# The diagonal of a recurrence's score matrix: from GpSimd products and two-column sums instead of full products

## The chip, the cores and the metric

The kernel runs on one core of a Trainium2 chip. The metric is the device time of one execution in microseconds (us). Engines are named as in the profile: PE is TensorE (matmuls; PEld its weight loads), DVE is VectorE, ACT is ScalarE, POOL is GpSimd, and SP is SyncE, whose queue issues most of the transfers. A tile of 128x512 has 128 partitions and 512 elements in each. PSUM is the memory that PE writes, SBUF the one that holds the operands.

## The reference

The program is two transformer blocks in a row on 512 tokens of width 1024, in float32. The first block mixes tokens by a stick-breaking attention and by a gated linear recurrence (HGRN2), then goes through a two-level mixture of 16 experts; the second has retention, a differential attention, a cross-attention and a dense feed-forward layer. The change concerns the recurrence alone. With eight heads of 64 key and 64 value elements, it is

```
cum = jnp.cumsum(gc, axis=2)                       # gc: log of the forget gate, in a chunk
diff = cum[:, :, :, None, :] - cum[:, :, None, :, :]
decay = jnp.exp(jnp.where(causal[:, :, None], diff, -jnp.inf))
scores = jnp.einsum('bhtk,bhsk,bhtsk->bhts', qc, kc, decay)
o = (jnp.einsum('bhts,bhsv->bhtv', scores, vc)
     + jnp.einsum('bhtk,bhkv->bhtv', qc * jnp.exp(cum), state))
```

The score of a query at t and a key at s is a sum over the key elements of q times k times a decay that differs for each element. On the diagonal, s = t, the decay is 1, and the score is the plain inner product of q and k at that token.

## The kernel before, in words

The program is written as one function, `body`; a scheduler then puts the instructions of each engine in a fixed order, and each engine works its own list from the front. An instruction that waits holds everything behind it on that engine. So a change of one operation can move others in the lists, and the order below is what the scheduler made of both programs.

The recurrence works on blocks of 128 tokens, four of them, and on pairs of heads, four pairs (`hgrn_pair(t)`, called for t = 0 to 3). A pair of heads fills the 128 partitions: head h holds partitions 64h to 64h + 63. For a pair, `hk[t]` holds the keys and `hc[t]` the running sums of the log gates, both 128x512; `hq[2t]` and `hq[2t + 1]` hold the queries of the two heads, each 128x512 with the other head's partitions filled with zeros, so that a product over 128 partitions gives one head alone.

The score matrix of a pair, transposed, is the tile `std`: 128 key positions, then 2 heads, 4 blocks and 128 query positions. It is built in two steps. First the diagonal: the lines 490 to 496 do, for each head, four full 128x128 products of keys and queries on PE into one PSUM bank, and VectorE multiplies the bank by the identity matrix `ident`, so that only the diagonal stays and the rest of `std` is zero. This product also gives the tile its zeros. Second, seven levels (m = 1, 2, 4, ..., 64) fill what lies under the diagonal. A level takes the decay against a reference position: VectorE makes the differences `e` (L506, L508), ACT their exponentials (L509, L512), VectorE the scaled keys `KT` (L510, L513) and the scaled queries `QT` (L516), PE multiplies them (L520), and the parts that belong to this level are put into `std`: by VectorE with a predicated copy (L523) for the first five levels, by ACT (L530) for the last two. After the levels come the state (L538 to L562), the output (L568, L570), and a norm over each head (L573 to L577, with the helper lines 311, 312, 319, 266 and 267).

The weights of all projections come through `split` (L180 to L183): a transfer on SP's queue into a buffer, then ACT rounds it (L182) and VectorE makes the rest (L183); three products of such parts (L200 to L202) stand for one exact product. While the recurrence runs, the scheduler puts pieces of the next projections (v, q and k of the stick-breaking attention) between its products on PE.

In this stretch GpSimd has eight fills with zeros (L591) and nothing else. PSUM tiles with the tag "at" share four banks here; `std` has two buffers.

Of the kernel before, what the change touches and what calls it, by code (L numbers as in the profile page):

```python
# [8 lines left out]
F32 = mybir.dt.float32  # L9
# [11 lines left out]
S = 512  # L21
# [62 lines left out]
def body(tc, a, out):  # L84
    nc = tc.nc
    V, A, T, G = nc.vector, nc.scalar, nc.tensor, nc.gpsimd
    es = ExitStack()

    def pool(name, bufs, side=None, space=None, stack=None):
        kw = {}  # L90
        if side:
            kw["side"] = side
        if space is not None:
            kw["space"] = space
        return (stack or es).enter_context(tc.tile_pool(name=name, bufs=bufs, **kw))
# [21 lines left out]
    def psum(tag, name="ps"):  # L117
        if tag == "at":
            return banks[1][0].tile([128, 512], F32, name=name, tag="at", bufs=banks[1][1])
        return ps.tile([128, 512], F32, name=name, tag=tag, bufs=2)  # L120
# [48 lines left out]
    ident = cp.tile([128, 128], F32, name="ident")  # L169
# [161 lines left out]
    ones64 = ones64r.bitcast(F32)  # L331
# [80 lines left out]
    at = ExitStack()  # L412
# [10 lines left out]
    hg = pool("hg", 1, side="right", stack=hgst)  # L423
# [9 lines left out]
    hq, hk, hc, hv = {}, {}, {}, {}  # L433
# [48 lines left out]
    def blocks(ap):  # L482
        return ap.rearrange("p (b t) -> p b t", b=4)
# [3 lines left out]
    def hgrn_pair(t):  # L487
        std = hg.tile([128, 2, 4, 128], F32, name="std", bufs=2)
        cum, k = hc[t], hk[t]
        tot = [cum[:, b * 128 + 127:b * 128 + 128] for b in range(4)]  # L490
        for h in range(2):
            o = blocks(psum("at"))
            for b in range(4):
                T.matmul(o[:, b, :], k[:, b * 128:(b + 1) * 128], hq[2 * t + h][:, b * 128:(b + 1) * 128],
                         start=True, stop=True)
            V.tensor_mul(std[:, h], o, ident[:, None, :].to_broadcast([128, 4, 128]))
        for lev, m in enumerate((1, 2, 4, 8, 16, 32, 64)):
            i = turn[0] % 2
            turn[0] += 1
# [14 lines left out]
            for h in range(2):  # L514
                p_ = slice(64 * h, 64 * h + 64)
                V.tensor_mul(Q_[p_, h, :].rearrange("p (g i) -> p g i", i=m),  # L516
                             halves(hq[2 * t + h], m)[p_, :, 1, :], ev[p_, :, 1, :])
            o = psum("at").rearrange("p (h t) -> p h t", h=2)
            for b in range(4):
                T.matmul(o[:, :, b * 64:(b + 1) * 64], K_[:, b * 128:(b + 1) * 128], Q_[:, :, b * 64:(b + 1) * 64],  # L520
                         start=True, stop=True)
# [23 lines left out]
        for h in range(2):  # L545
            p_ = slice(64 * h, 64 * h + 64)
# [9 lines left out]
        for b in range(3):  # L556
            for h in range(2):
                p_ = slice(64 * h, 64 * h + 64)
# [5 lines left out]
        o = psum("tp")  # L564
        for b in range(4):
# [3 lines left out]
            for h in range(2):  # L569
                T.matmul(o[64 * h:64 * h + 64, cc], hv[b][:, (2 * t + h) * 64:(2 * t + h + 1) * 64], std[:, h, b, :],  # L570
                         start=(b == 0), stop=(b == 3))
# [8 lines left out]
    for t in range(4):  # L580
        hgrn_pair(t)
# [880 lines left out]
```

## Time and profile before

| | us |
|---|---|
| median of 3 runs (1622.94 to 1624.32) | 1623.21 |
| the profiled execution | 1623.13 |
| its span, first to last instruction | 1621.3 |
| PE busy in the span | 1579.7 |
| DVE busy in the span | 955.9 |
| ACT busy in the span | 831.6 |
| POOL busy in the span | 75.2 |

The profiled execution's time is 1.8 us more than its span. The granted clock of PE was 0.998 of full speed over the run. A matmul is modelled as lasting longer than the time to the next one, since they are pipelined; that is why busy shares of PE near 100% do not say by themselves that PE is the bound, and why this document goes by what waits for what.

### The profile page before, as it was taken

The numbers are of one execution on the slowest core, as the hardware profiler recorded it, in microseconds if no ns is written. First come the engines' busy times: TensorE is split into PE (matmuls) and PEld (weight loads), VectorE is DVE, ScalarE is ACT, GpSimd is POOL, SyncE is SP. The second block draws the span as 40 slices with busy tenths as digits, with TensorE's granted clock in tenths as the row PEclk, the third lists the DMA queues.
The fourth block names the chain that finished last, engine by engine and source line by source line (L and its number), as shares of the span: only waits on it lengthen the run. The fifth ranks groups of instructions, "written<-read, shape, count | busy, mean of one in ns | idle before, by whom it ended". The sixth has DMA issues, their size and how long they took to land. (4 is left out here: it accounts for less than half of the span.)

```text
span 1621.3 us, 20374 instructions
## 1 busy us (share of the span) xinstructions
PE 1579.7 (97%) x7631; PEld 1223.8 (75%) x7631; DVE 955.9 (59%) x1485; ACT 831.6 (51%) x1331; POOL 75.2 (5%) x92
## 2 busy tenths in 40 slices
PE   7999999999999999999989999999999999999999
PEld 6887776668878777776667667657878888888887
DVE  6459945643647899998855766456555433333221
ACT  5445556665335888888865664434444322323120
POOL 3000000000001211111110000000000000000000
PEclk9999999999999999999999999999999999999999
DMA  7230121123469999999974204224211333332331
GB/s 227 72 104 27 53 79 39 48 67 119 143 231 317 310 369 368 357 365 368 380 263 135 75 15 130 75 58 142 90 53 54 115 91 105 91 103 92 97 124 39
DMA packets 203070, 242.88 MB, mean 150 GB/s; under 512 B 10400, under 2 KB 133560, under 8 KB 202968
## 3 DMA queue, kind: packets, MB, share of 16 engines
q1 hardware_dynamic: 188800, 205.43, 38.1%
q0 software_dynamic: 7056, 24.27, 5.3%
q10 hardware_dynamic: 7112, 11.85, 2.5%
q8 instruction: 61, 1.00, 0.2%
q14 instruction: 41, 0.34, 0.1%
HBM read 223.69 MB, written 15.73 MB: 148 GB/s over the span
## 5 line engine op out<-in xcount | busy, mean ns | idle before, releaser
L183 DVE TENSOR_TENSOR wlo<-wraw,whi 128x1024 fp32r<-128x1024 f32 x210 | 256.0, 1223 | 284.9 <-ACT whi L182 275.5
L182 ACT CAST whi<-wraw 128x1024 fp32r<-128x1024 f32 x210 | 220.5, 1051 | 392.9 <-PE ps L201 276.2
L200 PE MATMUL ps<-hTh,whi 128*128 128x512 f32 (+1 forms) x912 | 349.8, 384 | 1.3 <-DVE fsg L1412 0.8
L201 PE MATMUL ps<-hTl,whi 128*128 128x512 f32 (+1 forms) x912 | 348.4, 382 | 0.8 <-DVE hTl L267 0.8
L202 PE MATMUL ps<-hTh,wlo 128*128 128x512 f32 (+1 forms) x912 | 347.7, 382 | 0.0
L183 DVE TENSOR_TENSOR wlo<-rx,whi 128x1024 fp32r<-128x1024 f32 x176 | 210.4, 1221 | 36.6 <-ACT whi L182 34.2
L182 ACT CAST whi<-rx 128x1024 fp32r<-128x1024 f32 x176 | 182.7, 1049 | 52.5 <-PE ps L202 31.3
L200 PEld LDWEIGHTS ps<-hTh,whi 128*128 128x128 f32 x912 | 172.2, 189 | 36.6 <-issue 3.3
L201 PEld LDWEIGHTS ps<-hTl,whi 128*128 128x128 f32 x912 | 172.2, 189 | 33.4 <-issue 2.2
L202 PEld LDWEIGHTS ps<-hTh,wlo 128*128 128x128 f32 x912 | 172.1, 189 | 31.3 <-issue 0.3
L200 PE MATMUL ps<-whi,XT 128*96 128x512 f32 x256 | 101.5, 396 | 1.8 <-ACTq L1045 1.8
L202 PE MATMUL ps<-whi,XT 128*96 128x512 f32 x256 | 102.0, 398 | 0.0
L201 PE MATMUL ps<-wlo,XT 128*96 128x512 f32 x256 | 100.9, 394 | 0.0
L200 PE MATMUL ps<-whi,hTh 128*128 128x512 f32 x192 | 77.4, 403 | 0.3 <-ACT hTh L266 0.2
L202 PE MATMUL ps<-whi,hTl 128*128 128x512 f32 x192 | 77.4, 403 | 0.0
L201 PE MATMUL ps<-wlo,hTh 128*128 128x512 f32 x192 | 76.6, 399 | 0.0
L200 PE MATMUL ps<-whi,aTh 128*128 128x512 f32 x176 | 68.5, 389 | 0.0
L202 PE MATMUL ps<-whi,aTl 128*128 128x512 f32 x176 | 68.5, 389 | 0.0
L201 PE MATMUL ps<-wlo,aTh 128*128 128x512 f32 x176 | 68.5, 389 | 0.0
L1412 DVE TENSOR_TENSOR fsg<-fsg,ps 128x512 f32<-128x512 f32 x22 | 15.1, 688 | 76.4 <-PE ps L202 76.4
L200 PEld LDWEIGHTS ps<-whi,XT 128*96 128x96 f32 x256 | 41.4, 162 | 18.4 <-ACTq L1045 2.2
L201 PEld LDWEIGHTS ps<-wlo,XT 128*96 128x96 f32 x256 | 41.5, 162 | 17.4 <-DVE wlo L183 0.3
(449 smaller groups left out, 2590.6 us busy)
## 6 DMA issues: line engine op xcount, KB each, us to landing
wraw<-in_w_in_dram SPq DMA_DIRECT2D x72, 512.0 KB
rx<-in_w_exp_gate_dram SPq DMA_DIRECT2D x58, 512.0 KB
rx<-in_w_exp_down_dram SPq DMA_DIRECT2D x58, 512.0 KB
rx<-in_w_exp_up_dram SPq DMA_DIRECT2D x52, 512.0 KB
wraw<-in_w_gate_dram SPq DMA_DIRECT2D x22, 512.0 KB
wraw<-in_w_up_dram SPq DMA_DIRECT2D x22, 512.0 KB
wraw<-in_w_down_dram SPq DMA_DIRECT2D x22, 512.0 KB
wraw<-in_w_out_dram SPq DMA_DIRECT2D x16, 512.0 KB
```

The costliest lines, as they stand in the source:

```text
L182: i1 = A.copy(hi, w)
L183: i2 = V.tensor_sub(lo, w, hi.bitcast(F32))
L200: T.matmul(o, lh, rh, start=first, stop=False)
L201: T.matmul(o, lh, rl, start=False, stop=False)
L202: T.matmul(o, ll, rh, start=False, stop=last)
L1412: V.tensor_mul(sg[t], sg[t], o)
```

## The change

The diagonal is computed in another way. GpSimd multiplies keys and queries of each head element by element into one new tile `prod` (128x512, one buffer), each head on its own 64 partitions. PE then multiplies each block of `prod` by two columns of `ones64` (columns 0 and 64: a one for the partitions of head 0, a one for those of head 1), which sums the key elements of each head and leaves the diagonal as one column per head and block. ACT copies these eight columns out of PSUM into the new tile `dg`, and GpSimd multiplies the identity by them into the whole of `std`, 128x1024 at once. VectorE has no part in it any more.

```diff
@@ -488,12 +488,17 @@
         std = hg.tile([128, 2, 4, 128], F32, name="std", bufs=2)
         cum, k = hc[t], hk[t]
         tot = [cum[:, b * 128 + 127:b * 128 + 128] for b in range(4)]
+        prod = hg.tile([128, S], F32, name="prod", bufs=1)
         for h in range(2):
-            o = blocks(psum("at"))
-            for b in range(4):
-                T.matmul(o[:, b, :], k[:, b * 128:(b + 1) * 128], hq[2 * t + h][:, b * 128:(b + 1) * 128],
-                         start=True, stop=True)
-            V.tensor_mul(std[:, h], o, ident[:, None, :].to_broadcast([128, 4, 128]))
+            p_ = slice(64 * h, 64 * h + 64)
+            G.tensor_mul(prod[p_, :], k[p_, :], hq[2 * t + h][p_, :])
+        o = psum("at")
+        for b in range(4):
+            T.matmul(o[:, 2 * b:2 * b + 2], prod[:, b * 128:(b + 1) * 128], ones64[:, ::64], start=True, stop=True)
+        dg = hg.tile([128, 2, 4], F32, name="dg", bufs=2)
+        A.copy(dg, o[:, :8].rearrange("p (b h) -> p h b", h=2))
+        G.tensor_mul(std, ident[:, None, None, :].to_broadcast([128, 2, 4, 128]),
+                     dg[:, :, :, None].to_broadcast([128, 2, 4, 128]))
         for lev, m in enumerate((1, 2, 4, 8, 16, 32, 64)):
```

Lines behind this place have numbers higher by 5 in the changed program: its L528 is the predicated copy L523, its L515, L521 and L525 are L510, L516 and L520.

On GpSimd the list before the change, from the end of the zero fills of `hq` on, holds the fills of the next stage's queries only:

```order
L446 MEMSET hq_609 64x512
L446 MEMSET hq_612 64x512
L591 MEMSET sq_1697 64x512
L591 MEMSET sq_1700 64x512
L591 MEMSET sq_1767 64x512
```

In the changed program the same place reads as follows. The number behind a name tells copies of a tile apart: prod_911 and std_910 belong to pair 0, prod_1066 and std_1065 to pair 1, prod_1221 to pair 2.

```order
L446 MEMSET hq_609 64x512
L446 MEMSET hq_612 64x512
L494 ISA
L494 TENSOR_TENSOR prod_911<-hk_393,hq_498 64x512
L494 TENSOR_TENSOR prod_911<-hk_393,hq_501 64x512
L494 TENSOR_TENSOR prod_1066<-hk_396,hq_535 64x512
L494 TENSOR_TENSOR prod_1066<-hk_396,hq_538 64x512
L500 TENSOR_TENSOR std_910<-ident_103,dg_919 128x1024
L494 TENSOR_TENSOR prod_1221<-hk_430,hq_572 64x512
L494 TENSOR_TENSOR prod_1221<-hk_430,hq_575 64x512
L500 TENSOR_TENSOR std_1065<-ident_103,dg_1074 128x1024
```

The two products of the next pair stand ahead of the diagonal of the pair at hand. The first of them waits for PE, which reads the one buffer of `prod` in the sums of the pair at hand.

On VectorE the list before the change, where pair 1 begins its masked writes, reads:

```order
L496 TENSOR_TENSOR std_1066<-ps_1067,ident_103 128x512
L576 SCALAR_TENSOR_TENSOR sq_1061<-ps_1042,cols_221,rb_1058 128x512
L496 TENSOR_TENSOR std_1066<-ps_1073,ident_103 128x512
L577 TENSOR_TENSOR sq_1061<-sq_1061,hgt_286 128x512
L523 COPY_PREDICATED std_1066<-mk_282,ps_1085 128x512
L510 TENSOR_TENSOR KT0_898<-hk_396,e_1104 128x64x4
L267 TENSOR_TENSOR yhg1_269<-sq_1061,yhg0_268 128x512
```

And in the changed program:

```order
L521 TENSOR_TENSOR QT0_900<-hq_538,e_1102 64x256
L581 SCALAR_TENSOR_TENSOR sq_1060<-ps_1041,cols_221,rb_1057 128x512
L528 COPY_PREDICATED std_1065<-mk_282,ps_1083 128x512
L582 TENSOR_TENSOR sq_1060<-sq_1060,hgt_286 128x512
L528 COPY_PREDICATED std_1065<-mk_282,ps_1096 128x256x2
L515 TENSOR_TENSOR KT1_899<-hk_396,e_1115 128x32x8
L267 TENSOR_TENSOR yhg1_269<-sq_1060,yhg0_268 128x512
```

The two masked copies are gone, a KT and two QT of the third level stand ahead of the first predicated copy (the last of them is shown), and this copy now waits for GpSimd. Behind it stand the KT and QT of the further levels. PE's two-column sums stand where the full products stood, and ACT's copies into `dg` come in front of its other work of the pair. SP's list is unchanged. On every engine the lists are alike again when the recurrence is over.

## Rows read from the trace of the kernel before

**Rows 1.** Page, part 1: busy us, share of the span and instructions by engine.

```profile
PE 1579.7 (97%) x7631; PEld 1223.8 (75%) x7631; DVE 955.9 (59%) x1485; ACT 831.6 (51%) x1331; POOL 75.2 (5%) x92
```

**Rows 2.** Stretch of the recurrence: length, busy us by engine, clock, DMA share, GB/s.

```profile
107.00:212.00 105.00, 100.72 (x618) 80.42 (x618) 95.89 (x205) 54.72 (x96) 4.15 (x8) 1.00 0.14 41
```

**Rows 3.** Order of time, 120 to 122 us: start, length, engine, line, operation.

```profile
120.27 0.85 DVE L516 TENSOR_TENSOR QT<-hq,e 64x256 f32<-64x256 f32 x2
...
121.26 2.35 PE L520 MATMUL ps<-QT,KT 128*128 128x128 f32 x16
```

**Rows 4.** Waits of PE and DVE, 104 to 212 us: total us, times, longest.

```profile
PE ps L520 <- DVE QT L516: 3.7, 5, 1.0
...
DVE std L496 <- PE ps L494: 1.5, 3, 1.1
```

**Rows 5.** Waits of SP's queue over the span.

```profile
SPq L180 <- DVE wlo L183: 989.2, 168, 46.0
```

**Rows 6.** Groups of instructions, 104 to 212 us: busy us, mean ns | idle before.

```profile
L494 PE MATMUL ps<-hq,hk 128*128 128x128 f32 x64 | 7.8, 275 | 0.0
...
L496 DVE TENSOR_TENSOR std<-ps,ident 128x512 f32<-128x512 f32 x8 | 5.4, 686 | 1.5 <-PE ps L494 1.5
```

**Rows 7.** Order of time, 104 to 192 us, where each pair begins.

```profile
106.59 1.95 PE L494 MATMUL ps<-hq,hk 128*128 128x128 f32 x16
...
110.31 1.32 DVE L523 COPY_PREDICATED std<-mk,ps 128x512 f32<-128x512 uint8 x1
...
130.62 1.95 PE L494 MATMUL ps<-hq,hk 128*128 128x128 f32 x16
...
134.44 1.31 DVE L523 COPY_PREDICATED std<-mk,ps 128x512 f32<-128x512 uint8 x1
...
156.08 1.95 PE L494 MATMUL ps<-hq,hk 128*128 128x128 f32 x16
...
157.67 0.75 DVE L576 SCALAR_TENSOR_TENSOR sq<-ps,cols,rb 128x512 f32<-128x512 f32 x1
...
158.34 0.68 DVE L496 TENSOR_TENSOR std<-ps,ident 128x512 f32<-128x512 f32 x1
158.94 0.68 DVE L577 TENSOR_TENSOR sq<-sq,hgt 128x512 f32<-128x512 f32 x1
...
161.07 1.32 DVE L523 COPY_PREDICATED std<-mk,ps 128x512 f32<-128x512 uint8 x1
...
184.36 1.95 PE L494 MATMUL ps<-hq,hk 128*128 128x128 f32 x16
...
187.62 1.30 DVE L523 COPY_PREDICATED std<-mk,ps 128x512 f32<-128x512 uint8 x1
```

**Rows 8.** Order of time on PE, 510 to 512 us: products with few columns.

```profile
510.50 0.52 PE L898 MATMUL ps<-tw,eqs 128*96 128x6 bf16 x8
```

**Rows 9.** Groups of instructions on ACT, 107 to 212 us: a narrow operation.

```profile
L541 ACT ACTIVATE dec<-hc 128x2 f32<-128x2 f32 x2 | 0.4, 206 | 1.9 <-DVE ST L562 1.9
```

**Rows 10.** Groups of instructions on POOL, 35 to 440 us: fills.

```profile
L591 POOL MEMSET sq<- 64x512 f32 x8 | 4.1, 519 | 165.2 <-ACT std L530 89.2 <-DVE KT L539 49.7 <-ACT e L543 25.1
L760 POOL MEMSET hn<- 128x1024 f32 x1 | 1.0, 958 | 234.4 <-issue 234.4
```

**Rows 11.** Order of time on DVE, 67 to 69 us: keys of pair 0 finished.

```profile
68.08 0.40 DVE L466 TENSOR_SCALAR hk<-hk 128x512 f32<-128x512 f32 x1
```

**Rows 12.** Order of time on DVE and POOL, where fills run beside DVE.

```profile
124.25 0.52 POOL L591 MEMSET sq<- 64x512 f32 x1 [89.17 <-ACT std L530]
...
124.47 0.45 DVE L513 COPY KT<-hk 128x256 f32<-128x256 f32 x1
...
177.95 0.28 DVE L513 COPY KT<-hk 128x256 f32<-128x256 f32 x1
...
203.73 1.11 DVE L547 TENSOR_TENSOR qd<-hq,e 64x384 f32<-64x384 f32 x2
203.87 0.52 POOL L591 MEMSET sq<- 64x512 f32 x1 [0.59 <-DVE KT L539]
```

## Prediction

> **What bounds the kernel now.** I read the engines' totals first, then the stage of the change, then the waits inside it. TensorE (PE) is busy for 97% of the span [rows 1], so over the whole kernel it looks like the bound. The recurrence runs in the stretch from 107 to 212 us, and there the picture is different: VectorE (DVE) is busy 95.9 of 105 us, PE 100.7, ScalarE (ACT) 54.7, GpSimd (POOL) 4.2 [rows 2]. Who sets the pace is seen in the order of time. VectorE writes the QT of a level from 120.27 to 121.12 and PE starts on it at 121.26 [rows 3], 0.14 us later. Where PE comes too early it waits: 3.7 us in five places, all for QT. VectorE's waits for the removed products are 1.5 us in three places [rows 4]. So PE only fills its time with projections that the written order puts between the levels, and what VectorE loses or wins in this stage is handed on to PE almost in full.
>
> What follows the stage hands a shift on too. The loads on SyncE's queue wait 989 us in total, in 168 waits, for VectorE's split of a weight to free its buffer [rows 5]: the transfers are tied to the progress of the compute, not to a clock of their own. I take nothing off for later stages.
>
> **What goes.** PE loses 32 products of keys and queries, 64 instructions that took 7.8 us [rows 6]. VectorE loses eight masked copies of 0.69 us [rows 6]; the successor starts 0.60 us after one, at 158.94 after 158.34 [rows 7], so that 8 x 0.60 = 4.8 us of its queue go.
>
> **What comes on PE and ACT.** Sixteen products with two moving columns, two instructions each: 32. The trace has none in f32 with two columns. From below they cost 0.065 us each, by the bf16 products with six columns, of which eight take 0.52 us [rows 8]. From above they cost what the removed ones do, 7.8/64 = 0.12. I take 0.065, the nearer in columns: 2.1 us. PE's own work falls by 7.8 - 2.1 = 5.7 us (3.9 by the upper end). As VectorE sets the pace, this only lengthens PE's waits and is worth nothing by itself. ACT gets four narrow copies; a narrow operation takes 0.21 us [rows 9], 0.8 us together, under an engine that is idle half of the stage.
>
> **What comes on GpSimd.** Eight products of 64x512 and four of 128x1024, two operands read from SBUF each. GpSimd does no such operation before. Its fills of these sizes, which only write, take 0.52 and 0.96 us [rows 10]. That is the lower end. For the upper end I let each of three streams (two reads, one write) cost as much as a fill: 1.56 and 2.88. I take 1.2 and 2.2, a little over two streams.
>
> Where they stand matters more than their sum. The order of the changed program shows that GpSimd does the two products of the next pair ahead of the diagonal of this pair. The next pair's products need the buffer prod, which has one copy, so they wait until PE has read this pair's. All three therefore start when PE's two-column sums of this pair end, and the first masked write of VectorE (the predicated copy of its first level) waits for all three: 1.2 + 1.2 + 2.2 = 4.6 us in pairs 0 to 2, and 2.2 us in pair 3, whose products were done earlier. Together 3 x 4.6 + 2.2 = 16.0 us. The first pair's products are under cover: its hk is finished near 68.5 [rows 11], and PE asks for the sums near 106.6. Behind the waiting predicated copy stand the QT and KT of the next levels, and PE waits for those.
>
> What can VectorE do in these 16.0 us? Most of its work then reads two SBUF operands (e, KT, QT, splits). Whether it can run beside a GpSimd operation that reads SBUF no row shows. The nearest rows are a one-source copy: it took 0.45 us when a GpSimd fill of 0.52 us ran into it, and 0.28 without one; the two-operand products beside fills kept their length (1.11 us for two, 0.55 each) [rows 12]. So the two engines do stop each other for some operations. The upper bound is full exclusion; the lower is none.
>
> The Trainium skill, page "SBUF — State Buffer", section "SBUF: two separate sides", says that VectorE and GpSimd hold a shared port pair as an exclusive lock for a whole instruction, and that a VectorE operation with two SBUF inputs takes it against a GpSimd operation that reads SBUF. The copy and the fill agree with it; for two inputs no row here can, since GpSimd reads no tile in this kernel. By that rule exclusion is full.
>
> I take full exclusion, since this stage shows it where it can. Then VectorE loses the 16.0 us but for three things: its old waits in these places (1.5 us [rows 4]), the gain scaling of pairs 1 to 3, which reads PSUM and one SBUF tile and can run beside (its successor starts 0.67 us after it, at 158.34 after 157.67 [rows 7]: 3 x 0.67 = 2.0), and the masked copies that are gone (4.8). Sum: 16.0 - 1.5 - 2.0 - 4.8 = +7.7 us. With two streams per operation (1.04 and 1.92) it is 13.9 - 8.3 = +5.6, with three 20.9 - 8.3 = +12.6.
>
> The Trainium skill, page "GPSIMD Engine Reference", section "3.1 Elementwise — side-by-side cycle accounting", gives 4497 ns for an f32 product of 2048 elements. An estimate scaled from that page is 1.12 and 2.25 us here, and the sum by it would be 15.7 - 8.3 = +7.4; no run here shows it yet.
>
> The profiled execution took 1623.1 us, 1621.3 of span and 1.8 around it, and stands 0.1 below the median of 1623.2. So 1623.1 + 7.7 = **1630.8 us**.
>
> **The rivals.**
> A, the forecast: exclusion, 1628.7 to 1635.8 by the two ends.
>
> B, no exclusion; only the new wait counts. VectorE works on until the predicated copy and then waits. PE started the removed products at 106.59, 130.62, 156.08 and 184.36; I let the sums end 0.5 us after that (eight instructions of 0.065). The diagonal is then there at 111.7, 135.7, 161.2 and 187.1, against 110.31, 134.44, 161.07 and 187.62 where the copy starts before [rows 7]: +1.4, +1.3, +0.1, -0.5. Work that the new order puts ahead of the copy or behind it changes these to about +1.0, +0.6, +0.9 and -1.3 (a two-operand step of 0.35 to 0.60 us each). Sum +1.2: 1624.3. For it: the two-operand steps beside fills kept their length. Against it: a fill reads nothing.
>
> C, faster: GpSimd is near its lower end (0.52 and 0.96 us, 2.0 for the three) and does not hold VectorE up. Then the diagonal is there 2.0 us after the sums, before the copy wants it (at 109.1 against 110.31), and VectorE's queue is shorter by 4.8 us, which PE, with 5.7 us less to do, can follow: 1618.3. For it: VectorE is the pace of the stage, and 4.8 us of it really go. Against it: an operation with two operands as cheap as a fill.
>
> D, GpSimd above three streams, for the operands that repeat an element along a row: each further us in the four diagonals costs 4 us, past 1636.
>
> E, nothing happens because PE is the bound of the stage after all: then the 5.7 us of PE work would be won, 1617.4. The 0.14 us between QT and PE speaks against it.
>
> **How the numbers follow.** A 0.53, B 0.17, C 0.21, D 0.05, E 0.04. A measurement of this kernel can tell about 0.2% (3.2 us) from no change. A and D are slower by more than that; a tenth of B's spread is slower as well. C and E are faster, and B is the same: slower 0.59, same 0.16, faster 0.25. The likeliest case alone is 1628.7 to 1635.8. The range goes down to half of C: 1618 to 1636.
>
> **What would show it.** On GpSimd: eight products near 1.2 us, four near 2.2, in groups of three that end with the first predicated copy of a pair. On VectorE: a wait of that copy for GpSimd, and steps of 0.42 us that take a microsecond beside GpSimd. PE's wait for QT and for what follows from it should grow from 3.7 to about 3.7 + 7.7 + 5.7 = 17.1 us, and the stage should end some 8 us later. If VectorE's steps keep their length beside GpSimd, B or C is right; if the copy never waits for GpSimd, the whole argument is wrong. If the later stages do not end later by what this one does, my carrying the shift to the end is wrong.

## The result and the profile after

The changed kernel takes 1639.67 us in the median of six runs (1636.28 to 1643.01), the kernel before 1623.62 on the same chip (six runs): ratio 1.0100, with a 95% interval of 1.0088 to 1.0112. It is slower by 16.0 us where 7.7 were forecast, and 3.7 us past the upper end of the range. The direction was right, the size half of what came.

The profiled execution of the changed kernel took 1643.01 us, 1641.2 of span. GpSimd's list in it, in order of time (start, length, engine, line, operation, count, and in brackets the idle time before it with what ended it):

```profile
69.47 3.71 POOL L494 TENSOR_TENSOR prod<-hk,hq 64x512 f32<-64x512 f32 x2 [34.39 <-DVE hk L466]
112.40 3.68 POOL L494 TENSOR_TENSOR prod<-hk,hq 64x512 f32<-64x512 f32 x2 [39.22 <-ACT whi L182]
116.16 1.96 POOL L500 TENSOR_TENSOR std<-ident,dg 128x1024 f32<-128x1024 f32 x1
142.37 2.69 POOL L494 TENSOR_TENSOR prod<-hk,hq 64x512 f32<-64x512 f32 x2 [24.25 <-PE ps L497]
145.14 1.96 POOL L500 TENSOR_TENSOR std<-ident,dg 128x1024 f32<-128x1024 f32 x1
...
171.26 3.74 POOL L494 TENSOR_TENSOR prod<-hk,hq 64x512 f32<-64x512 f32 x2 [9.82 <-PE ps L497]
175.08 1.90 POOL L500 TENSOR_TENSOR std<-ident,dg 128x1024 f32<-128x1024 f32 x1
...
203.12 1.90 POOL L500 TENSOR_TENSOR std<-ident,dg 128x1024 f32<-128x1024 f32 x1 [24.98 <-ACT rb L312]
```

The groups of three are there, and they take 5.7, 4.7 and 5.7 us from the first start to the last end, then 1.9 alone: 18.0 us where 16.0 were forecast. VectorE beside them, same kernel and view:

```profile
69.57 1.39 DVE L518 COPY KT<-hk 128x256 f32<-128x256 f32 x1
70.88 1.21 DVE L465 TENSOR_TENSOR_SCAN hc<-seg,lf 128x512 f32<-128x512 bf16 x1
72.01 1.45 DVE L466 TENSOR_SCALAR hk<-hk 128x512 f32<-128x512 f32 x1
...
112.27 1.23 DVE L183 TENSOR_TENSOR wlo<-wraw,whi 128x1024 fp32r<-128x1024 f32 x1 [4.20 <-ACT whi L182]
113.41 1.51 DVE L515 TENSOR_TENSOR KT<-hk,e 128x256 f32<-128x256 f32 x1
114.84 1.52 DVE L521 TENSOR_TENSOR QT<-hq,e 64x256 f32<-64x256 f32 x1
118.15 1.28 DVE L528 COPY_PREDICATED std<-mk,ps 128x512 f32<-128x512 uint8 x1 [1.79 <-POOL std L500]
...
143.85 3.53 DVE L521 TENSOR_TENSOR QT<-hq,e 64x256 f32<-64x256 f32 x2
```

A KT takes 1.51 us, two QT take 3.53; the two QT of [rows 3] took 0.85. The shape is that of taking turns: the two products beside the split at 112.27 take 3.68 us, about a split (1.23) more than the two at 142.37 (2.69, so 1.34 each). The KT ends at 114.92 and the QT at 116.36, just behind the second product, which ends at 116.08. The second QT could not even start: the masked copy stands ahead of it and waits for the diagonal.

PE in the same place, in order of time:

```profile
111.22 0.95 PE L497 MATMUL ps<-ones64r,prod 128*128 128x2 f32 x8
112.03 2.03 PE L525 MATMUL ps<-QT,KT 128*128 128x128 f32 x16
...
119.94 2.07 PE L525 MATMUL ps<-QT,KT 128*128 128x128 f32 x8 [3.83 <-DVE QT L521]
...
147.52 1.13 PE L525 MATMUL ps<-QT,KT 128*128 128x128 f32 x8 [2.88 <-DVE QT L521]
...
181.79 2.35 PE L525 MATMUL ps<-QT,KT 128*128 128x128 f32 x16 [3.48 <-DVE QT L521]
...
209.93 1.13 PE L525 MATMUL ps<-QT,KT 128*128 128x128 f32 x8 [2.66 <-ACT sq L597]
```

The stretches around the first of these gaps in the same kernel, and those behind the second and the third (stretch and length; busy us of PE, PEld, DVE, ACT and POOL with their counts; then PE's granted clock, DMA share, GB/s):

```profile
118.00:120.00 2.00, 0.06 (x1) 0.06 (x1) 1.79 (x3) 0.00 (x0) 0.11 (x1) 0.69 0.00 0
120.00:122.00 2.00, 2.00 (x9) 2.00 (x10) 1.78 (x3) 0.00 (x0) 0.00 (x0) 0.50 0.00 0
122.00:124.00 2.00, 2.00 (x7) 1.52 (x6) 1.91 (x5) 0.00 (x0) 0.00 (x0) 0.50 0.00 0
124.00:126.00 2.00, 2.00 (x11) 1.90 (x10) 0.68 (x3) 1.26 (x2) 0.00 (x0) 0.60 0.00 0
...
148.00:150.00 2.00, 2.00 (x13) 1.74 (x13) 2.00 (x4) 0.07 (x1) 0.00 (x0) 1.00 0.00 0
...
182.00:184.00 2.00, 1.91 (x17) 1.75 (x17) 1.96 (x6) 0.00 (x0) 0.00 (x0) 1.00 0.00 0
```

PE stands idle for 3.83 us, its clock falls from the upper of its two levels (2.4 GHz) to the lower (1.2), and eight products take 2.07 us, as long as the sixteen at 112.03 (2.03). Such stretches lie also near 78 us, behind a gap of 2.23 us, and near 212, behind the one of 2.66. But not every long gap does this: behind those of 2.88 and 3.48 us the granted clock is 1.00. PE's waits between 104 and 230 us (total, times, longest), beside [rows 4]:

```profile
PE ps L525 <- DVE QT L521: 11.8, 6, 3.8
PE ps L525 <- ACT sq L597: 2.7, 1, 2.7
```

What this amounts to can be counted. GpSimd's fill of hn is its first work behind the recurrence, and serves here as the mark of the recurrence's end and the projections beside it. In the kernel before:

```profile
438.81 0.96 POOL L760 MEMSET hn<- 128x1024 f32 x1 [234.43 <-issue]
```

In the changed kernel:

```profile
454.28 0.97 POOL L765 MEMSET hn<- 128x1024 f32 x1 [232.00 <-issue]
```

The stretches up to that mark, columns as above, in the kernel before:

```profile
60.00:104.00 44.00, 43.93 (x194) 36.08 (x193) 20.26 (x29) 19.46 (x28) 0.00 (x0) 1.00 0.31 96
104.00:215.00 111.00, 106.72 (x646) 85.42 (x645) 97.65 (x208) 56.26 (x97) 4.15 (x8) 1.00 0.17 48
215.00:438.81 223.81, 220.74 (x988) 164.38 (x988) 117.67 (x197) 125.00 (x244) 0.00 (x0) 1.00 0.25 76
```

And in the changed kernel:

```profile
60.00:104.00 44.00, 41.77 (x178) 34.08 (x177) 21.58 (x29) 18.29 (x27) 3.63 (x2) 0.96 0.28 85
104.00:215.00 111.00, 96.33 (x545) 77.33 (x544) 89.08 (x175) 50.05 (x88) 20.73 (x16) 0.95 0.15 43
215.00:454.28 239.28, 236.40 (x1078) 175.81 (x1077) 130.17 (x223) 132.72 (x259) 1.04 (x2) 1.00 0.25 76
```

The fill comes 15.5 us later, close to the loss of 16.0 in the medians: the rest of the program hands it on. (The profiled execution, the slowest of the six, lost 19.9; its further 4.4 us lie behind the mark, and no trace shows whether the other five have them.) PE's idle time is length less busy: 0.1 + 4.3 + 3.1 before, 2.2 + 14.7 + 2.9 after, 12.4 more. After 215 us PE idles for 3 us either way. So until the fill comes, what VectorE loses counts only where PE idles for it.

### The profile page after: what moved, and what is told of

It reads as the page before. It is cut to its first block, busy times and chain, and to the rows that moved or that the text cites. A ratio compares the mean times of both kernels' runs of the same rounds, so it can differ in the third digit from the quotient of the medians.

```text
span 1641.2 us, 20302 instructions
## 1 busy us (share of the span) xinstructions
PE 1583.9 (97%) x7599; PEld 1224.7 (75%) x7599; DVE 960.8 (59%) x1477; ACT 831.5 (51%) x1335; POOL 97.2 (6%) x104
## 5 line engine op out<-in xcount | busy, mean ns | idle before, releaser
L201 PEld LDWEIGHTS ps<-wlo,XT 128*96 128x96 f32 x256 | 41.4, 162 | 18.6 <-DVE wlo L183 1.6
## 6 DMA issues: line engine op xcount, KB each, us to landing
rx<-in_w_exp_up_dram SPq DMA_DIRECT2D x52, 512.0 KB, 12.2
```

The source lines that it names most:

```text
L201: T.matmul(o, lh, rl, start=False, stop=False)
```

## The experiments

The theory after the result, called exclusion: GpSimd's reads of SBUF and VectorE's steps shut each other out, PE starves, and its clock falls on top. Its rivals: the new chain (products, sums, diagonal, masked copy) costs by its length alone; the clock costs nothing. Each kernel was timed beside the kernel before (median near 1623 us).

**The first pair's products later (e_late0).** They wait for the last value tile and so leave the scans at 69 us alone.

```diff
-            G.tensor_mul(prod[p_, :], k[p_, :], hq[2 * t + h][p_, :])
+            i_ = G.tensor_mul(prod[p_, :], k[p_, :], hq[2 * t + h][p_, :])
+            if t == 0: order(i_, gate)     # gate: a copy of one column of hv[3]
```

> The changed kernel, but GpSimd's products of pair 0 wait until the last v tile (hv[3]) is there, near 84 us, and so no longer run beside VectorE's scans. Theory A (GpSimd operations that read SBUF and VectorE's two-operand or two-port operations stop each other, and the first two products beside the scans delayed ACT's copy of v, so that PE waited 2.2 us and then ran at half clock for 3.4 us): about 4 us less than the changed kernel, 1635 to 1636 us; a copy of 0.29 us and a scaling of 0.40 us that took 1.39 and 1.45 in the changed kernel are back at 0.3 and 0.4, and PE does not wait for hv. Rival B (only the wait of the first predicated copy for the diagonal counts, because three GpSimd operations stand in a row): nothing changes, 1639 to 1640.

Measured: 1636.33, ratio 1.0086 [1.0073, 1.0099]; fill of hn at 450.22, 4.1 us earlier than in the changed kernel. VectorE's key copy and key step at 69 to 73 us, 1.39 and 1.45 us in the changed kernel, are back at 0.29 and 0.40, and PE's idle 2.2 us there and 1.7 us of lost clock are gone. So "under cover" was wrong for these two products.

**Fills instead of products and diagonals (e_fills)**, and **three fills each (e_fills3)**, so that GpSimd works in the same places, in e_fills3 as long as with the products, but reads next to nothing. The diagonal's values are left out.

```diff
-            G.tensor_mul(prod[p_, :], k[p_, :], hq[2 * t + h][p_, :])
+            # copies of one column of k and hq, then two (e_fills3: three) times
+            G.memset(prod[p_, :], 0.01)
-        G.tensor_mul(std, ident..., dg...)
+            # a copy of one column of dg, then two (e_fills3: three) times
+            G.memset(std, 0.0)
```

> The changed kernel with GpSimd's products replaced by fills of about the same length (two fills of 0.52 us for each 64x512 product, two of 0.96 for the diagonal) behind narrow copies of one column that keep what they wait for. It leaves out the diagonal's values. GpSimd then has nearly the same time and the same waits but reads no tile. Theory A (exclusion): the steps of VectorE keep 0.42 us, the first predicated copy waits less, PE's idle stretches fall under what cost it the clock; about 1625 to 1628. Rival B (only the chain through GpSimd counts, now 4.2 us a pair): 1634 to 1638, close to the changed kernel.

> Each product of the changed kernel is replaced by three fills of the same tile (about 1.56 us) and the diagonal by three fills of std (about 2.9 us), each behind a copy of one column that keeps the order; the diagonal's values are left out. GpSimd is busier than in the changed kernel, but reads next to nothing. Exclusion theory: VectorE's eviction copies keep their 0.42 to 0.49 us, and only the longer chain product, sums, std adds: 1620.4 (with one fill each) plus at most 4 x 2 us, so 1621 to 1628. Rival, that GpSimd's length alone makes the loss: 1636 to 1642, as the changed kernel or more.

Measured: 1620.44, ratio 0.9984 [0.9976, 0.9993], below both forecasts for it, and 1622.46, ratio 0.9993 [0.9984, 1.0002], inside that of exclusion. With three fills each, VectorE in the first pair:

```profile
109.16 0.42 DVE L525 TENSOR_TENSOR KT<-hk,e 128x256 f32<-128x256 f32 x1
109.50 0.85 DVE L531 TENSOR_TENSOR QT<-hq,e 64x256 f32<-64x256 f32 x2
110.38 0.42 DVE L525 TENSOR_TENSOR KT<-hk,e 128x256 f32<-128x256 f32 x1
110.72 0.84 DVE L531 TENSOR_TENSOR QT<-hq,e 64x256 f32<-64x256 f32 x2
...
114.34 2.66 DVE L538 COPY_PREDICATED std<-mk,ps 128x512 f32<-128x512 uint8 x2 [1.32 <-POOL std L510]
```

GpSimd works from 107.99 to 114.31 here, longer than the 5.7 us of the changed kernel, and no step beside it is longer than before; the masked copy still waits. The scheduler also put more of VectorE's steps ahead of that copy than in the changed kernel, so part of what the wait costs is hidden by order; that a KT takes 0.42 and not 1.51 us is not. The rival of length alone falls. Without the reads (e_fills) the change is 2.5 us faster than before, about half of what rival C had.

**No diagonal at all (e_none)**: std is filled with zeros, the diagonal is left out.

```diff
-        # products, sums, dg, diagonal
+        G.memset(std, 0.0)
```

> The kernel before without any diagonal: the products of keys and queries and the masked copies are left out, and std is filled with zeros by GpSimd well ahead. This is what the change could win at most. Theory A (VectorE sets the pace of the recurrence): 4.8 us less than before, 1618.5 to 1619.5. Rival (PE sets it): 7.8 us less, 1615.8. Rival (neither, the stage waits for something else): 1623.

Measured: 1615.62, ratio 0.9953 [0.9939, 0.9966], which is 7.3 us less than the kernel before beside it (interval 5.5 to 9.9). That is the figure of the rival that PE sets the pace (1615.8), not that of VectorE (1618.5 to 1619.5). The fill of hn comes at 433.40, 5.4 us earlier, with PE's idle time alike (7.3 against 7.4): it is PE's own work that went. PE's list in the kernel before, behind the products at 106.59 [rows 7], goes on with

```profile
108.38 1.84 PE L520 MATMUL ps<-QT,KT 128*128 128x128 f32 x15
```

So the old products held PE for 1.79 us a pair, 7.2 in all. The two-column sums of the changed kernel hold it for 0.81 (from 111.22 to 112.03), 3.2 in all: 3.9 us of the list are saved. By the fill of hn 3.1 are (e_fills); where the other 0.8 stays is open.

**Diagonals on ScalarE (e_stda)**, products in place. ScalarE makes eight scaled copies of ident.

```diff
-        G.tensor_mul(std, ident..., dg...)
+        for h in range(2):
+            for b in range(4):
+                A.activation(std[:, h, b, :], ident, AF.Copy, scale=dg[:, h, b:b + 1])
```

> The changed kernel, with the diagonal put into std by ScalarE (eight scaled copies of ident a pair) and not by GpSimd; the products stay where they are. Exclusion theory: the four diagonals held GpSimd for 1.9 us each, of which 1 to 1.5 us stood in VectorE's way and then PE's; without them 4 to 7 us come back: 1632 to 1636. Rival, that the products alone make the whole loss or that ScalarE's copies are as late: 1638 to 1641.

Measured: 1625.32, ratio 1.0017 [1.0008, 1.0025]: 14 us less than the changed kernel, twice what was expected. The products still stretch VectorE:

```profile
112.94 1.50 DVE L516 TENSOR_TENSOR KT<-hk,e 128x256 f32<-128x256 f32 x1
114.37 1.94 DVE L522 TENSOR_TENSOR QT<-hq,e 64x256 f32<-64x256 f32 x2
```

but the gap of PE behind them is 1.40 us, and the granted clock is 1.00 from 104 to 215 us. Here too the scheduler put more of VectorE's steps ahead of the masked copy.

**All products ahead of the levels.** In two buffers with ScalarE's diagonals (e_act), in four buffers with these (e_act2), and in four buffers with GpSimd's diagonals (e_early2).

```diff
+    for t in range(4):       # before the levels, behind a copy of a column of hv[3]
+        prod = hg.tile(...)  # e_act: two buffers; else also sq and rb, tiles of the norm not yet in use
+        # both products of pair t, its sums on PE, its dg on ScalarE
```

> GpSimd makes the products of all four pairs behind hv[3], from about 84 us on, where VectorE is idle half of the time; PE's sums and ACT's copies of the eight columns follow at once; the diagonal is put into std by ACT, eight scaled copies of the identity a pair, so GpSimd does nothing that reads SBUF during the levels. Theory A: VectorE's 4.8 us are won and nothing stops it, ACT (54.7 of 105 us busy) has room for 10 us more: 1619 to 1621, below both kernels. Rival C (the new order of the lists on PE and VectorE is what costs): 1630 or more. Rival D (ACT's copies become late and take the place of GpSimd's): 1624 to 1628.

> All four pairs' products run on GpSimd after hv[3], with four separate buffers, so that they are done before the first pair's levels begin at about 107 us; the sixteen sums follow in PE's order at about 106 us, and ScalarE builds each diagonal as eight scaled copies of ident. GpSimd reads nothing during the levels. Exclusion theory: no VectorE instruction of the levels is stretched, PE has no half-clock stretch between 107 and 212 us; PE loses about what the kernel without a diagonal lost not, that is 1615.6 plus 3.2 us for the sums (16 x 0.2 us): 1617 to 1621, faster than before (ratio about 0.998), POOL's fill for hn at 435 to 438 us. Rival: the sums or ScalarE's eight copies a pair set the pace, and it comes out as with two buffers, 1624 to 1626, with PE waiting for std.

> As the kernel with all products ahead of the levels in four buffers (1620.0), but the diagonals on GpSimd, not on ScalarE. Their sums are there before the levels begin and std has two buffers, so that a diagonal is written a pair ahead and nothing waits for it; it only reads SBUF beside VectorE. With the other three versions this makes a table of two by two: products early or in place, diagonals on ScalarE or GpSimd. If it is the exclusion alone that costs, four diagonals of 1.9 us each take up to 7.7 us from VectorE: 1624 to 1628. If it is the wait of the first masked copy for the diagonal that makes most of the 14 us between the changed kernel and the one with ScalarE's diagonals, this comes out at 1619 to 1622. If the two edits simply add up, wait or no wait, 1632 to 1635.

Measured: e_act 1624.34, ratio 1.0009 [1.0000, 1.0018]; e_act2 1620.00, ratio 0.9981 [0.9972, 0.9990]; e_early2 1625.64, ratio 1.0018 [1.0009, 1.0027]. e_act missed the time of its theory: with two buffers half of the products could only run at 108.75, beside the levels (6.42 us for four). PE waited 1.78 us for them and then ran at half clock for 10 us. (The time is that forecast for late copies of ScalarE, but it was the products that came late.) e_act2 has GpSimd done in time:

```profile
86.17 6.30 POOL L586 TENSOR_TENSOR prod<-hk,hq 64x512 f32<-64x512 f32 x4
92.55 3.52 POOL L586 TENSOR_TENSOR sq<-hk,hq 64x512 f32<-64x512 f32 x2
96.14 3.52 POOL L586 TENSOR_TENSOR rb<-hk,hq 64x512 f32<-64x512 f32 x2
```

It leaves nothing of the computation out and beats both kernels, by 3 and by 20 us. Its clock was not as expected: it fell for 3.4 us without a gap, behind all 32 instructions of the sums in a row.

```profile
106.68 1.84 PE L591 MATMUL ps<-ones64r,prod 128*128 128x2 f32 x16
...
109.27 1.03 PE L591 MATMUL ps<-ones64r,rb 128*128 128x2 f32 x8
110.17 0.69 PE L200 MATMUL ps<-whi,hTh 128*128 128x512 f32 x1
```

e_early2 came within the first forecast for it (exclusion without a wait).

Four versions make a table, by PE's idle time from 104 to 215 us: e_act2 2.7; products in place alone (e_stda) 5.7; GpSimd's diagonals alone (e_early2) 5.9; both (the change) 14.7. Each alone adds 3 us, together 12: a short stop of VectorE passes under the fill work between PE's levels, and a stop of 5.7 us in a row, as the one buffer of prod and the order on GpSimd make it, does not. That reading is argued from the gaps and not shown, since VectorE's order is not the same in the four; the idle times are measured.

**Work in PE's gap (e_bridge, e_bridge2).** e_late0 with matmuls that nobody reads between the first pair's levels 1 and 2, where PE idled for 3.83 us.

```diff
+            if t == 0 and lev == 2:   # e_bridge2: 16, behind a product that reads QT
+                for r_ in range(14):
+                    T.matmul(osum[:, 8:512], ones64r, hT[0][:, r_ % 8, 0:504], start=True, stop=True)
```

> The kernel with the first pair's products behind hv[3] (1636.3), and 14 matmuls of 504 columns whose result nobody reads, between the first pair's products of level 1 and level 2, where PE had idled for 3.8 us before its granted clock fell to 0.5. Clock theory: PE is not idle there, the stretch at half clock behind it (6.8 us, 3.4 us of work) goes, and the recurrence ends about 3 us earlier: 1632.5 to 1634.5. Rival, the clock is not what costs or does not answer to that gap: 1636 to 1639.5, since the added matmuls (3.2 us) end later than the wait did.

> The kernel with the first pair's products behind hv[3] (1636.3), and between the first pair's products of level 1 and level 2 one product and 16 matmuls of 504 columns whose result nobody reads; they start behind the first half of level 2's QT (about 112.4 us) and end near 116, where level 2 could start in any case, so that four or five of the fill matmuls stay ahead of them and the rest go behind. Clock theory: PE does not idle for 3.8 us, the half-clock stretch of 6.8 us behind that place goes, and what PE won (3.4 us) less the fills put off (at most 1 us) shows at the end of the recurrence: POOL's fill for hn at 447 to 448.5 us, not 450.2, time 1633 to 1635. Rival, the clock falls in spite of the work, or its fall costs nothing because VectorE sets the pace there: 450 us or later, 1636 to 1638.

e_bridge settled nothing: 1640.34, ratio 1.0108 [1.0093, 1.0122], outside both forecasts. The scheduler took the nine fill matmuls (the projections that e_late0 has in this place) away, the added ones ended at 112.1, a gap of 2.70 us was left and behind eight products another of 1.27, and the clock fell there. In e_bridge2 they reach the next level:

```profile
111.72 0.46 PE L530 MATMUL ps<-QT,KT 128*128 128x128 f32 x2 [1.27 <-DVE QT L526]
111.94 3.89 PE L534 MATMUL ps<-hTh,ones64r 128*128 128x504 f32 x16
115.67 1.05 PE L538 MATMUL ps<-QT,KT 128*128 128x128 f32 x8
```

The eight products of level 2 take 1.05 us, not 2.08 as in e_late0: with the gap filled, the clock stays up there. But the time is 1635.56, ratio 1.0077 [1.0063, 1.0090], 0.8 us less than e_late0, and the fill of hn comes at 449.95: far from the 447 to 448.5 of the clock theory and at the edge of what the rival had (450 or later). At the first pair's state product PE was 2.6 us ahead (127.55 against 130.12 us). Then it gave this back: the added work holds PE for 4.0 us (111.72 to 115.67) in which it did none of the projections, so that these were still to do. Its clock also fell behind gaps of 2.87 and 3.55 us further on, where e_late0 has gaps of 2.88 and 3.49 with the clock at 1.00. Against e_late0, idle time changes by -2.4, lost clock by -1.7 and work by +4.0, in sum -0.1, and the fill comes 0.3 earlier. So the time of this pair of runs alone decides nothing about the rival that the fall costs nothing; the account below, over all kernels, speaks against it.

## Why the prediction was wrong

**The account.** Up to the fill of hn, PE has work in its list for nearly every gap (7.4 us idle from 60 us on in the kernel before). Its end moves by PE's idle time (length less busy), plus what it loses at half clock (the sum over stretches of 2 us of length times one less the granted clock), plus work added, less the 3.1 us of PE work saved (e_fills, whose idle time and clock are those of before):

| kernel | idle | clock | work | sum | fill of hn, measured |
|---|---|---|---|---|---|
| after | +12.4 | 6.9 | -3.1 | +16.2 | +15.5 |
| e_late0 | +10.2 | 5.1 | -3.1 | +12.2 | +11.4 |
| e_stda | +3.5 | 1.7 | -3.1 | +2.1 | +2.8 |
| e_early2 | +1.6 | 3.4 | -3.1 | +1.9 | +2.6 |
| e_act | +0.2 | 5.1 | -3.1 | +2.2 | +2.4 |
| e_fills3 | +1.4 | 1.7 | -3.1 | 0.0 | -0.6 |
| e_act2 | -1.6 | 1.7 | -3.1 | -3.0 | -3.3 |
| e_bridge2 | +7.8 | 3.4 | -3.1 + 4.0 | +12.1 | +11.1 |
| e_bridge | +11.5 | 6.8 | -3.1 + 3.4 | +18.6 | +16.5 |

Seven of the nine come out within 0.8 us, with one constant from a tenth kernel; the two with added work 1.0 and 2.1 too high. Where PE idles while its clock is low, the table counts that time twice (0.6 us in the changed kernel). Leave the clock out and the changed kernel comes to +9.3, 6.2 short, e_late0 4.3 and e_act 5.3. So a clock that falls takes its share of PE's list here. That a kept clock would give all of it back is not shown: no two runs differ in the clock alone. The table says where PE's time went; why PE idled is what the runs with fills, with later products and with ScalarE's diagonals show.

Now the forecast in the same terms. It said that PE's waits grow by 7.7 + 5.7 = 13.4 us and its work falls by 5.7, together +7.7.

**Right: exclusion (A), and the idle time that comes of it.** The steps of VectorE are stretched beside reads and not beside fills; idle grew by 12.4 for the 13.4. That these are so close is in part luck: in the levels, where the forecast put all of it, idle grew by 10.4, and 2.2 came from the first pair's products, which it put at nothing. The Trainium skill, page "SBUF — State Buffer", section "SBUF: two separate sides", was weighed for this: the traces agree, with 1.51 us against 0.42 for a KT, and also with its condition that only a GpSimd operation that reads SBUF shuts out a two-input step. Rivals B and C (no exclusion) fall with the stretched steps, D (GpSimd above three streams) with GpSimd's rows: 1.34 and 1.9 us for the forecast 1.2 and 2.2. (The upper end of A is 1623.1 + 12.6 = 1635.7, not 1635.8; nothing hangs on it.) The estimates from the page "GPSIMD Engine Reference" of the Trainium skill, section "3.1 Elementwise — side-by-side cycle accounting", were 1.12 and 2.25, scaled from a figure that the page gives for an addition; against 1.34 and 1.93 each is 16% off, in opposite directions, and the measurement decides.

**Wrong, 6 to 7 us: no price for PE's clock.** The prediction turned PE's waits into time one to one. It had a wait of 4.6 us of VectorE per pair in its own sum and did not ask what the granted clock does behind such a gap. The row in the result (3.83 us idle, then 0.50) and the row of e_bridge2 show it. From the lengths of the gaps alone it could not have been summed: of the five long gaps of the changed kernel, three brought the clock down and two did not. The Trainium skill, page "TensorE: Matmul & The Clock Gate", section "Terms", prices time at the lower level by the share of pulses that is not passed: half of it. The traces agree: eight products took 2.08 us in e_late0 at the lower level and 1.05 in e_bridge2 at the upper.

**Wrong, 2.6 us: the work saved on PE.** The forecast saved 7.8 - 2.1 = 5.7. The 7.8 us of busy time [rows 6] are 7.2 us of PE's list, since matmuls overlap, and the sums take 3.2: 0.10 us an instruction, near the 0.12 of the removed products and not the 0.065 taken from the bf16 ones. That saves 3.9, the upper end of the cost that the prediction named and did not choose; the fill of hn shows 3.1.

**Wrong in reason: "worth nothing by itself".** e_fills and e_none won PE's work with PE's idle time as before. VectorE sets when a level can start; PE, with projections to fill the gaps, sets when the stretch ends. Rival E, held at 0.04, had this right and missed the exclusion.

**Wrong: "under cover".** The first pair's products met the scans and key steps of the pairs behind it: 4.1 us (e_late0), of which 1.7 is clock; both parts are contained in the idle and clock terms above.

The misses are 6.2 to 6.9 (clock) and 2.6 (work), less 1.0 of idle forecast too high: 7.8 to 8.5, against 15.5 - 7.7 = 7.8. That later stages hand the shift on was right.

## What to carry to other kernels

Where one engine has work for nearly every gap, count in its terms: what the change adds to its idle time and its work, and what its clock may give up behind a long gap. Give that last term a range, from nothing to the loss behind each gap. Moving work to GpSimd beside a busy VectorE costs both engines when GpSimd reads SBUF; the same products put ahead of the busy stretch, and the diagonal on ScalarE, made a change that lost 16 us gain 3. An operation that finishes early is under cover only if the engine that it shuts out has nothing on the path then.

## What was not expected of the hardware

One-input steps are shut out too: a float32 copy of 128x256 took 1.39 us beside a product (0.28 to 0.45 [rows 12]), a scaling of 128x512 1.45 (0.40 [rows 11]). GpSimd is held up in turn: 3.7 us for two products beside a split or a scan, 2.69 else. PE's granted clock fell to 0.50 behind gaps of 2.23, 2.66 and 3.83 us and stayed at 1.00 behind gaps of 2.88 and 3.48 in the same execution; in e_bridge2 it fell behind 2.87 and 3.55, and in e_act2 behind 32 instructions with two columns and no gap. So the length of a gap alone did not decide it here. ScalarE's eight scaled copies of 128x128 took 2.45 us in e_stda, against GpSimd's 1.93 for the diagonal, and the steps of VectorE beside them kept 0.42 us.
